# Layer 0's first modulation, norms and projections in a hand-written order with their loads, and the mLSTM gates issued behind the first queries

## The chip, the cores and the metric

The kernel runs on one core of one Trainium2 chip. The metric is the device time of one execution in microseconds (us), and of several executions the median is taken. Engines are named as the profile names them: PE multiplies matrices, DVE is the vector engine, ACT the scalar engine, POOL the GpSimd engine, SP issues the DMAs. PSUM is the accumulator memory of PE, in eight banks of 512 fp32 columns on 128 partitions.

## The reference, cut to what matters

Two layers of a transformer that is modulated by a conditioning vector work on 1024 latent tokens and 256 context tokens of width 1024. The change touches the beginning of layer 0 alone:

```python
mod_l = (jax.nn.silu(c) @ ada_w[layer] + ada_b[layer]).reshape(batch, 1, N_MOD, D_MODEL)
mod_c = (jax.nn.silu(c_ctx) @ ada_w[layer] + ada_b[layer]).reshape(1, 1, N_MOD, D_MODEL)
h_l = modulate(x, norm1_g[layer], mod_l, 0)      # rms_norm(x, g) * (1 + mod[1]) + mod[0]
h_c = modulate(ctx, norm1_g[layer], mod_c, 0)
y_c, y_l = ab_mixer(h_c, h_l, ab_w_in[j], ab_gate_b[j], mlstm_norm_g[j], swa_q_norm_g[j],
                    swa_k_norm_g[j], swa_sink[j], ab_w_out[j], not last)
```

`ab_mixer` projects the modulated tokens to mLSTM gates, mLSTM heads, and the queries, keys and values of a banded attention. An mLSTM gate is a running sum and a running maximum along the tokens.

## The kernel before, in words

**Layout and groups.** Activations lie with the channel on the partition: `x[j]`, j = 0 to 7, holds 128 channels of all 1280 tokens. Tokens go in three groups, 0 and 1 of 512 and 2 of 256. Every projection is done in about twice the precision of one pass: activation and weight are split in a high and a low part (`hhi`, `hlo`, and a weight's two halves), and three matmuls are added up per 128 channels (high by high, low by high, high by low). With three groups, eight chunks j and two weight units (G for the gates and KB for the keys) that is 96 matmuls of 512 columns and 48 of 256 in the first stage.

**The first stage**, `first` (L2246 to L2284), has four kinds of work.

- Modulation, `ada_quarter(q)` (L229): quarter q gives shift and scale of the chunks j = 2q and 2q+1. It loads four tiles of `ada_w` (two DMAs of 256 KB each, L241) into a ring of slots s0f to s5f called raw, multiplies them by the conditioning vector (L244), copies one half of the result out of PSUM on ACT (L249), adds the other on DVE (L251), turns the sums to the partition axis by 16 small matmuls (L255), and adds the bias and forms the scale `gs` on DVE (L262, L267). No chunk of a quarter can be modulated before its L267.
- Statistics, `norm_stats` (L306), per group: eight squares on ACT (L312), added up in a tree of five additions on DVE and two on POOL (L315), one matmul with ones (L300), then Ln and Exp on ACT (L302, L303), which give the reciprocal root `rs`.
- Modulated chunk, `norm_apply` (L356): DVE multiplies `x`, `gs` and `rs` (L364), ACT adds the shift and writes `hhi` (L369). For an even j DVE then writes `hlo` (L374); for an odd j ACT writes the full value (L371) and POOL subtracts (L372). The scratch of squares and chunks is one ring of five buffers.
- Projection (L2281): six matmuls per chunk.

The weight units come by L395 and are split by ACT (L378) and POOL (L379); a third unit, V, is split there too, into the tiles mrv and irv.

**What sets the order.** Both before and after, an engine executes its instructions in one fixed order and waits on semaphores. Before, the framework's scheduler chose that order for the whole kernel from the order in which the Python code issues the work. `first` issued four rounds q = 0 to 3: load and square group q, modulation quarter q, then all chunks that this quarter allows for the groups at hand.

**What comes next.** `mixer0` (L1218) goes on with the keys, the values, and then with the queries and the mLSTM heads, whose projections are L404 to L406, with evacuations at L449 (ACT), L450 (DVE) and L478 (DVE, after the squares' matmul L475). It issued `gates` (L1119) ahead of the first queries. `gates` computes its scans on DVE (L1156 to L1179), four exponentials per direction on ACT (L1197, L1199), and for each of the two directions 14 small matmuls into PSUM banks 3 and 5 (L1206 and L1211), each bank copied out by DVE (L1207, L1215) before it is filled again. L1382 is a score matmul of the attention.

Of the kernel before, what the change touches and what calls it, by code (L numbers as in the profile page):

```python
# [10 lines left out]
F32 = mybir.dt.float32  # L11
F32R = mybir.dt.float32r
# [7 lines left out]
P = 128  # L20
D = 1024
ND = D // P
CTX = 256
LAT = 1024
T = CTX + LAT
# [3 lines left out]
TGS = [(256, 512, 0), (768, 512, 0), (0, 256, 1)]  # L29
# [17 lines left out]
PG = 1024  # L47
# [49 lines left out]
class Kernel:  # L97
# [128 lines left out]
            )  # L226
        yield

    def ada_quarter(self, q, tp, psp):  # L229


        nc, a = self.nc, self.a
        acc = tp.tile([P, 512], F32, tag="adaacc")
        for kk in range(2):
            ps = psp.tile("D", "adaps")
            for e in range(2):
                w = tp.tile([P, 2, 2, 256], F32, tag="raw")
                k0 = 4 * kk + 2 * e
                src = a["ada_w"][0, k0 * P : (k0 + 2) * P, 0:2048].rearrange("(k p) (b n) -> p k b n", p=P, b=2)
                for b in range(2):  # L240
                    nc.sync.dma_start(w[:, :, b, :], src[:, :, b, q * 256 : q * 256 + 256])  # L241
                for i in range(2):
                    c = 2 * e + i
                    nc.tensor.matmul(  # L244
                        ps[32 * c : 32 * c + 32, :], self.cs[:, k0 + i, :], w[:, i, :, :].rearrange("p b n -> p (b n)"),
                        start=True, stop=True, tile_position=(0, 32 * c),
                    )
            if kk == 0:
                nc.scalar.activation(acc, ps, AF.Copy)  # L249
            else:  # L250
                nc.vector.tensor_tensor(acc, ps, acc, op=ALU.add)  # L251
        pt = psp.tile("D", "adapt")
        for i in range(4):
            for u in range(2):
                nc.tensor.matmul(  # L255
                    pt[:, 2 * i : 2 * i + 2], acc[:, i * P : (i + 1) * P], self.asel[:, 2 * u : 2 * u + 2],
                    start=u == 0, stop=u == 1,
                )
        j = slice(2 * q, 2 * q + 2)
        bc = lambda t: t.unsqueeze(2).to_broadcast([P, 2, 2])  # L260
        ab = self.v(V_AB, 16).rearrange("p (b i) -> p b i", b=2)[:, :, j]
        nc.vector.tensor_tensor(  # L262
            self.mod[0][:, :16, :].rearrange("p (b i) v -> p b i v", b=2)[:, :, j, :],
            pt[:, :8].rearrange("p (b i v) -> p b i v", b=2, v=2),
            ab.unsqueeze(3).to_broadcast([P, 2, 2, 2]), op=ALU.add,
        )
        nc.vector.scalar_tensor_tensor(  # L267
            self.gs[0, 1][:, j, :], self.mod[0][:, 8 + 2 * q : 10 + 2 * q, :], 1.0, bc(self.v(V_N1 + 2 * q, 2)),
            op0=ALU.add, op1=ALU.mult,
        )  # L270
# [947 lines left out]
    def mixer0(self, first):  # L1218
        nc, a = self.nc, self.a
        cp = self.cp  # L1220
        dr = self.pool(self.ctx, "dr0", space=DRAM)
        mixd = [dr.tile([P, T], F32, tag=f"m0_{k}", name=f"m0_{k}") for k in range(ND)]
        ud = [[dr.tile([P, T], F32, tag=f"u{h}{i}", name=f"u{h}{i}") for i in range(4)] for h in range(4)]
        tri = cp.tile([P, 2, P], BF16, tag="tri", name="tri")
        idb = cp.tile([P, P], BF16, tag="idb", name="idb")
        sel = cp.tile([P, 2, 8], F32R, tag="sel", name="sel")
        with ExitStack() as ctx:
            kp = self.pool(ctx, "kp", side="right")
            with ExitStack() as c2:
                sp = self.sp = self.pool(c2, "sp")  # L1230
                small = Area(sp.tile([P, 640], F32, tag="small", name="small"))
                wp = self.weights_ring((0, 1), (0, PG))
                gy, heads = first(wp, kp)
                psp = self.banks(A=(0, 1), B=(2, 3), Q=(4,), S=(5,))
                tp = self.area(6 * PG, 8 * PG)
                self.qt_bufs = 1
                tr = tp.tile([P, 512], F32, tag="qsw")[:, : 2 * P].rearrange("p (d q) -> p d q", d=2)
                nc.sync.dma_start(tr, a["tri"].rearrange("d p q -> p d q"))
                nc.vector.tensor_copy(tri, tr)
                nc.vector.tensor_copy(idb, self.ident)  # L1240
                selc = small.tile([P, 1], F32, tag="selc")
                for d in range(2):
                    for h in range(4):
                        k = d * 4 + h
                        r = 64 * d + h
                        nc.vector.tensor_tensor(
                            selc, self.ident[:, r : r + 1], self.ident[:, r + 32 : r + 33], op=ALU.add
                        )
                        for i in range(2):
                            nc.vector.tensor_scalar(sel[:, i, k : k + 1], selc, (-1.0, 1.0)[i], None, op0=ALU.mult)  # L1250
                tb = self.area(5 * PG, 6 * PG)
                psa = self.banks(A=(0, 1, 2), B=(7,), Q=(4,), G=(3, 5))
                st, qs = self.swa_setup(sp, tp, tb, psa, wp, heads, gy)
                mr, ir, cb, tq = self.gates(kp, small, psa, gy)
                for _ in st[-1](psa, 0, qs):
                    pass
                self.gps = self.banks(A=(6, 7))
                heads = [self.gather(wp, tb, ud, h) for h in range(4)]
                for _ in range(7):
                    next(heads[0])  # L1260
                self.gps = psp
                self.swa(sp, small, tb, psp, wp, mixd, heads, st, qs)
                keep = self.area(NF - 320)
                kept = []
                for t in (cb, tq):
                    k = keep.tile(list(t.shape), F32, tag=f"k{len(kept)}")
                    nc.vector.tensor_copy(k, t)
                    kept.append(k)
            self.stage_weights()
            self.mlstm(mr, ir, *kept, tri, idb, sel, mixd, ud)  # L1270
        hb = self.hb = self.pool(self.ctx, "hb", side="right").tile([P, 5 * H], F32R, tag="hb", name="hb")
        self.hid = Area()
        self.hid_places = cuts(self.hidA, H, 0, H, 2 * H) + cuts(hb, H, *(i * H for i in range(5)))
        self.hid.place("hid", self.hid_places)
        self.make_gs(0, 2)
        self.new_h()
        return self.out_proj0(mixd)
# [954 lines left out]
def body(ctx: ExitStack, tc: tile.TileContext, a, out):  # L2232
    nc = tc.nc
# [12 lines left out]
    def first(wp, kp):  # L2246
# [1 line left out]

        sl = [k.sp.tile([P, T], F32, tag=f"s{i}", name=f"s{i}f") for i in range(7)]
        tp = k.area(2 * PG)  # L2250
        tp.place("raw", [x[:, :PG] for x in sl[:6]])
        tp.place("adaacc", cuts(k.F, H, 6 * PG))
        ps = k.banks(N=(0, 1, 2), G=(0, 1, 2), K=(3, 5, 6), D=(4, 7))
        k.nrs_bufs, k.nt_bufs = 3, 5
        k.gs[0, 1] = k.cp.tile([P, ND, 2], F32, tag="gs01", name="gs01")
        rs, heads, w = {}, {}, []
        for q in range(4):
            if q < 3:
                k.load_x(a["x"], TGS[q : q + 1], 0)
                rs[q] = k.norm_stats(TGS[q], tp, ps, "N")  # L2260
            if q == 0:
                w = [k.unit(wp, a["win0"][u]) for u in (U_G, U_KB)]
                hl = [kp.tile([P, T], F32R, tag=x, name=x + "v")[:, :PG] for x in ("mr", "ir")]
                heads["v"] = k.unit(wp, a["win0"][U_VB], place=(k.F[:, 7 * PG : 8 * PG], *hl))
            k.ada_quarter(q, tp, ps)
            todo = [(i, 2 * q, 2 * q + 2) for i in range(min(q, 2))]
            if q < 3:
                todo.append((q, 0, 2 * q + 2))
            else:
                todo.append((2, 6, 8))  # L2270
            for i, j0, j1 in todo:
                k.norm_apply(TGS[i], rs[i], 0, 1, tp, range(j0, j1))
                t0, n, vv = TGS[i]
                if t0 not in heads:
                    heads[t0] = [ps.tile(x, "pj") for x in "GK"]
                for j in range(j0, j1):
                    c = slice(j * P, j * P + P)
                    hi, lo = (t[:, j, t0 : t0 + n] for t in (k.hhi, k.hlo))
                    for o, (wh, wl) in zip(heads[t0], w):
                        for m, (x, y) in enumerate(((wh, hi), (wh, lo), (wl, hi))):  # L2280
                            nc.tensor.matmul(  # L2281
                                o[:, :n], x[:, c], y, start=j == 0 and m == 0, stop=j == ND - 1 and m == 2
                            )
        return sl[6], heads  # L2284

    nt = k.area(5 * PG, NF)
# [41 lines left out]
```

## Time and profile before

| what | value |
|---|---|
| median of three runs | 2880.11 us (2876.76 to 2883.9) |
| the profiled execution | 2882.76 us, of which the span of the trace is 2881.0 us |
| granted TensorE clock, mean | 0.981 of full speed |
| instructions | 41902 |
| DMA traffic | 432.11 MB, mean 150 GB/s |

The page gives busy time per engine over the span; the timeline view gives start, duration, engine, line, operation and operands of single instructions, with the idle time ahead of them and what released them in brackets; the windows view gives busy time per stretch, in which PEclk is the granted clock. A few per cent of PE records can be missing.

### The profile page before, as it was taken

To read this page: it belongs to the slowest core of one execution; us is meant where nothing else is said; L and a number is where in the kernel's file an instruction comes from. 1 tells how busy PE (TensorE), PEld (TensorE's weight loads), DVE (VectorE), ACT (ScalarE), POOL (GpSimd) and SP (SyncE) were. 2 spreads that over 40 slices of the span, in tenths; PEclk is the share of its full clock that TensorE was granted. 3 is DMA by queue.
4 is the path that set the end of the run, shared out by engine and by line. 5 is a ranking of instruction groups with operands and counts; after the bars stand their busy time and mean duration, and the time that the engine had idled before them with its cause. 6 is when DMAs were issued, how large, how long until landed. Compare 5 with 4: busy or idle time off the path is not lost.

```text
span 2881.0 us, 41902 instructions
## 1 busy us (share of the span) xinstructions
PE 2745.3 (95%) x15174; PEld 2334.7 (81%) x15174; DVE 1992.4 (69%) x3285; ACT 1503.1 (52%) x2640; POOL 1160.9 (40%) x768
## 2 busy tenths in 40 slices
PE   6889999999898999989999998999989999999999
PEld 3678788878787888878878898999988888888877
DVE  5836555667869877746777836888885567766766
ACT  5555554445654334344346645888875555544332
POOL 3431220110326666550001654777775299840000
PEclk9889999999999999999999999999999999999999
DMA  6113223352324566669765831000026245577674
GB/s 231 61 50 103 79 97 136 112 194 80 119 92 136 179 210 212 201 211 332 244 208 161 264 124 32 27 19 27 20 77 218 88 150 199 189 254 270 213 226 154
DMA packets 200368, 432.11 MB, mean 150 GB/s; under 512 B 21216, under 2 KB 46944, under 8 KB 200160
## 3 DMA queue, kind: packets, MB, share of 16 engines
q1 hardware_dynamic: 200160, 429.43, 45.2%
q8 instruction: 119, 1.95, 0.3%
q14 instruction: 89, 0.73, 0.1%
HBM read 326.85 MB, written 102.50 MB: 149 GB/s over the span
## 4 chain that ended last, share of the span: by engine, by line
PE 55%; DVE 12%; DMA 8%; issue 7%; ACT 4%; POOL 4%; SPq 0%; DVEq 0%; POOLq 0%; ACTq 0%
PE psum L998 12%; PE psum L569 12%; DMA hhiraw<-in_w 4%; PE psum L406 4%; PE psum L404 4%; PE psum L405 4%; PE psum L1924 4%; PE psum L2112 3%; PE psum L1830 3%; DVE W L379 3%; POOL W L379 2%; DVE F L623 1%; DVE F L211 1%; PE psum L1091 1%; DVE x L1003 1%
## 5 line engine op out<-in xcount | busy, mean ns | idle before, releaser
L379 POOL TENSOR_TENSOR W<-F,W 128x512 fp32r<-128x512 f32 (+2 forms) x323 | 516.5, 1614 | 524.9 <-ACT W L378 398.3
L998 PE MATMUL psum<-W,W 128*128 128x512 f32 x2688 | 622.7, 393 | 14.5 <-DVE W L379 6.4
L998 PEld LDWEIGHTS psum<-W,W 128*128 128x128 f32 x2688 | 506.5, 189 | 130.4 <-DVE W L379 15.8
L569 PE MATMUL psum<-hhi,W 128*128 128x512 f32 (+1 forms) x1600 | 449.3, 361 | 16.3 <-DVE x L623 7.0
L378 ACT ACTIVATE W<-F 128x512 fp32r<-128x512 f32 (+2 forms) x380 | 273.7, 739 | 250.7 <-POOL F L542 98.4
L569 PEld LDWEIGHTS psum<-hhi,W 128*128 128x128 f32 x1600 | 289.5, 192 | 63.3 <-DVE x L623 8.8
L569 PE MATMUL psum<-hlo,W 128*128 128x512 f32 (+1 forms) x800 | 287.2, 359 | 0.0
L378 ACT ACTIVATE W<-hhiraw 128x1024 fp32r<-128x1024 f32 x98 | 103.9, 1061 | 326.3 <-PE psum L998 252.6
L404 PE MATMUL psum<-hhi,W 128*128 128x512 f32 (+1 forms) x624 | 233.0, 373 | 6.6 <-DVE F L478 6.6
L406 PE MATMUL psum<-hhi,W 128*128 128x512 f32 (+1 forms) x624 | 228.1, 366 | 1.3 <-POOL W L379 1.3
L405 PE MATMUL psum<-hlo,W 128*128 128x512 f32 (+1 forms) x624 | 227.8, 365 | 0.0
L924 DVE TENSOR_TENSOR hhiraw<-hhiraw 128x512 f32<-128x512 f32 x154 | 105.2, 689 | 127.0 <-DMA hhiraw<-in_w 120.2
L372 POOL TENSOR_TENSOR hlo<-F,hhi 128x512 fp32r<-128x512 f32 (+1 forms) x28 | 35.0, 1254 | 361.2 <-ACT F L371 357.4
L542 POOL TENSOR_TENSOR F<-F 128x512 f32<-128x512 f32 x112 | 170.2, 1520 | 17.4 <-DMA F<-in_w 10.3
L569 PEld LDWEIGHTS psum<-hlo,W 128*128 128x128 f32 x800 | 153.7, 192 | 21.5 <-issue 0.2
L379 DVE TENSOR_TENSOR W<-hhiraw,W 128x1024 fp32r<-128x1024 f32 x98 | 119.6, 1221 | 46.2 <-ACT W L378 46.1
L404 PEld LDWEIGHTS psum<-hhi,W 128*128 128x128 f32 x624 | 119.2, 191 | 27.4 <-DVE F L478 7.0
L406 PEld LDWEIGHTS psum<-hhi,W 128*128 128x128 f32 x624 | 118.9, 191 | 18.6 <-POOL W L379 1.7
L405 PEld LDWEIGHTS psum<-hlo,W 128*128 128x128 f32 x624 | 119.3, 191 | 16.9 <-issue 1.7
L569 PE MATMUL psum<-x,W 128*128 128x512 f32 x504 | 123.5, 390 | 0.0
L581 ACT ACTIVATE F<-F 128x512 f32<-128x512 f32 x82 | 51.3, 626 | 134.9 <-DVE F L623 134.9
L379 DVE TENSOR_TENSOR W<-hloraw,W 128x1024 fp32r<-128x1024 f32 x98 | 119.4, 1219 | 0.1
(432 smaller groups left out, 6533.3 us busy)
## 6 DMA issues: line engine op xcount, KB each, us to landing
F<-in_w SPq DMA_DIRECT2D x104, 512.0 KB, 4.4
hloraw<-hd SPq DMA_DIRECT2D x90, 512.0 KB, 4.8
hhiraw<-in_w SPq DMA_DIRECT2D x72, 512.0 KB, 4.1
hd<-F SPq DMA_DIRECT2D x142, 256.0 KB, 2.2
hhiraw<-in_w SPq DMA_DIRECT2D x116, 256.0 KB, 5.4
F<-in_ada_w SPq DMA_DIRECT2D x96, 256.0 KB, 3.3
hd<-x SPq DMA_DIRECT2D x90, 256.0 KB, 2.3
F<-in_win SPq DMA_DIRECT2D x33, 512.0 KB, 3.7
```

The source lines that it names most:

```text
L378: nc.scalar.activation(hi, src, AF.Copy)
L379: eng.tensor_tensor(lo, src, hi.bitcast(F32), op=ALU.subtract)
L404: nc.tensor.matmul(ps, sh, mh, start=i == 0, stop=False)
L405: nc.tensor.matmul(ps, sh, ml, start=False, stop=False)
L406: nc.tensor.matmul(ps, sl, mh, start=False, stop=i == n - 1)
L542: add = lambda o, p, q, how: nc.gpsimd.tensor_tensor(o, p, q, op=how)
L569: nc.tensor.matmul(ps, w[i][:, p], B[j][k], start=first and j == 0 and m == 0, stop=last and j == 3 and m == 2)
L924: tt = lambda o, p, q, how: eng.tensor_tensor(o, p, q, op=how)
L998: nc.tensor.matmul(bank(base + i), A[u][:, p], B[v], start=first and m == 0, stop=last and m == 2)
L1830: nc.tensor.matmul(ps, s[:, c], m[:, j, t0 : t0 + QT], start=j == 0 and i == 0, stop=j == ND - 1 and i == 2)
L1924: nc.tensor.matmul(u.o[:, :QT], v[x], p[y], start=c == 0 and m == 0, stop=c == 2 * NB - 1 and m == 2)
L2112: self.nc.tensor.matmul(ps, x[:, c], y, start=first and m == 0, stop=last and m == 2)
```

## The change

`ada_quarter` is split: `ada_load(i)` issues the two DMAs of tile i (i = 0 to 15), and `ada_quarter(q, ws)` does the rest with four tiles already issued. The raw ring has seven slots instead of six. The body of `first` stands under `manual_schedule` for all five engines, so that its instructions run in the order written. In `mixer0`, the call of `gates` moves from ahead of the first queries to behind them and behind seven steps of the first head's gathering. No computation is added or left out. The rest of the kernel is still ordered by the scheduler.

```diff
+        def load(n):
+            for _ in range(n):
+                tiles.append(k.ada_load(next(number), tp))
...
+        with k.tc.manual_schedule(engines={E.PE, E.DVE, E.Activation, E.Pool, E.SP}):
+            k.load_x(a["x"], TGS[:1], 0)
+            stats(0)
+            w = [k.unit(wp, a["win0"][u]) for u in (U_G, U_KB)]
+            load(7)
+            raw = k.F[:, 7 * PG : 8 * PG]
+            nc.sync.dma_start(raw, a["win0"][U_VB])
+            k.load_x(a["x"], TGS[1:2], 0)
+            ada(0)
+            load(4)
+            k.load_x(a["x"], TGS[2:], 0)
+            apply(0, 0, 2)
+            ada(1)
+            load(4)
+            project(0, 0, 2)
+            apply(0, 2, 4)
+            v = heads["v"] = [kp.tile([P, T], F32R, tag=x, name=x + "v")[:, :PG] for x in ("mr", "ir")]
+            k.split(*v, raw, nc.gpsimd)
+            project(0, 2, 4)
+            stats(1)
+            apply(1, 0, 4)
+            ada(2)
+            load(1)
+            project(1, 0, 4)
+            for i in range(2):
+                apply(i, 4, 6)
+                project(i, 4, 6)
+            stats(2)
+            apply(2, 0, 6)
+            ada(3)
+            project(2, 0, 6)
+            for i in range(3):
+                apply(i, 6, 8)
+                project(i, 6, 8)
...
                 st, qs = self.swa_setup(sp, tp, tb, psa, wp, heads, gy)
-                mr, ir, cb, tq = self.gates(kp, small, psa, gy)
                 for _ in st[-1](psa, 0, qs):
                     pass
                 self.gps = self.banks(A=(6, 7))
                 heads = [self.gather(wp, tb, ud, h) for h in range(4)]
                 for _ in range(7):
                     next(heads[0])
+                mr, ir, cb, tq = self.gates(kp, small, psa, gy)
```

Line numbers in the rows of after are five higher than before for the functions behind `ada_quarter` (L312 becomes L317, L1211 becomes L1216).

On ACT, in the first stage, the squares of group 1 (x_116 to x_123) stood before between the first chunks of group 0:

```order
L249 ACTIVATE F<-psum 128x512
L312 ACTIVATE F<-x_116 128x512
L312 ACTIVATE F<-x_117 128x512
L369 ACTIVATE hhi<-F,mod_80 128x512
L312 ACTIVATE F<-x_118 128x512
L369 ACTIVATE hhi<-F,mod_80 128x512
L312 ACTIVATE F<-x_119 128x512
L371 ACTIVATE F<-F,mod_80 128x512
```

They stand now behind the copy of the second quarter (the second L254), the chunks that need it, and the high part of V (mrv):

```order
L254 ACTIVATE F<-psum 128x512
L374 ACTIVATE hhi<-F,mod_80 128x512 x2
L376 ACTIVATE F<-F,mod_80 128x512
L383 ACTIVATE mrv<-F 128x1024
L317 ACTIVATE F<-x_116 128x512
L317 ACTIVATE F<-x_117 128x512
L317 ACTIVATE F<-x_118 128x512
```

So a square of group 1 runs only when quarter 1 is done and its two chunks of group 0 are written.

On PE, behind the last of the key projections, the small matmuls of the gates (L1206, L1211) stood before closely one after another, between query projections:

```order
L1206 MATMUL psum<-x_808,ident 128x10 x4
L1211 MATMUL psum<-ident,x_808 128x128 x8
L406 MATMUL psum<-hhi,W_104 128x512
L404 MATMUL psum<-hhi,W_104 128x512
L475 MATMUL psum<-F,blk 128x512
L405 MATMUL psum<-hlo,W_104 128x512
L406 MATMUL psum<-hhi,W_104 128x512
L1211 MATMUL psum<-ident,x_808 128x128 x2
L475 MATMUL psum<-F,blk 128x512
L1211 MATMUL psum<-ident,x_808 128x128 x2
L1206 MATMUL psum<-x_808,ident 128x10 x4
L1211 MATMUL psum<-ident,x_808 128x128 x8
```

They stand now some 120 matmuls later, and the query and head projections (L409 to L411) stand ahead of them; of their second direction this is the beginning:

```order
L1216 MATMUL psum<-ident,x_1120 128x128 x2
L1384 MATMUL psum<-KH_627,x_813 128x256
L1385 MATMUL psum<-KL_629,x_813 128x256
L1384 MATMUL psum<-KH_627,x_814 128x256
L1385 MATMUL psum<-KL_629,x_814 128x256
L409 MATMUL psum<-hhi,W_103 128x512
L1211 MATMUL psum<-x_1120,ident 128x10 x4
L1216 MATMUL psum<-ident,x_1120 128x128 x2
L410 MATMUL psum<-hlo,W_103 128x512
L411 MATMUL psum<-hhi,W_103 128x512
```

Between the first direction's transposes and these stand 24 projection matmuls. The number of instructions on each engine is the same in both programs, and the order of all engines is the same from PE's 684th matmul on (DVE's 209th instruction, ACT's 184th, POOL's 59th).

More of the change, by code (lines that the diff above doesn't have):

```diff
@@ L227, in ada_sums, with ada_load, ada_quarter @@
         yield
-    def ada_quarter(self, q, tp, psp):
-        nc, a = self.nc, self.a
+    def ada_load(self, i, tp):
+        q, k0 = i // 4, 2 * (i % 4)
+        w = tp.tile([P, 2, 2, 256], F32, tag="raw")
+        src = self.a["ada_w"][0, k0 * P : (k0 + 2) * P, 0:2048].rearrange("(k p) (b n) -> p k b n", p=P, b=2)
+        for b in range(2):
+            self.nc.sync.dma_start(w[:, :, b, :], src[:, :, b, q * 256 : q * 256 + 256])
+        return w
+    def ada_quarter(self, q, ws, tp, psp):
+        nc = self.nc
         acc = tp.tile([P, 512], F32, tag="adaacc")
@@ L236, in ada_quarter @@
             for e in range(2):
[L237 to L241, printed above, removed]
+                w, k0 = ws[2 * kk + e], 4 * kk + 2 * e
                 for i in range(2):
@@ L2250, in first @@
         tp = k.area(2 * PG)
-        tp.place("raw", [x[:, :PG] for x in sl[:6]])
+        tp.place("raw", [x[:, :PG] for x in sl])
         tp.place("adaacc", cuts(k.F, H, 6 * PG))
@@ L2255, in first @@
         k.gs[0, 1] = k.cp.tile([P, ND, 2], F32, tag="gs01", name="gs01")
[L2256 to L2283, printed above, removed]
@@ new lines, in first, with stats, ada, apply @@
+        rs, heads, tiles = {}, {}, deque()
+        number = iter(range(16))
+        def load(n):
+            for _ in range(n):
+                tiles.append(k.ada_load(next(number), tp))
+        def stats(i):
+            rs[i] = k.norm_stats(TGS[i], tp, ps, "N")
+        def ada(q):
+            k.ada_quarter(q, [tiles.popleft() for _ in range(4)], tp, ps)
+        def apply(i, j0, j1):
+            k.norm_apply(TGS[i], rs[i], 0, 1, tp, range(j0, j1))
+        def project(i, j0, j1):
+            t0, n, vv = TGS[i]
+            if t0 not in heads:
+                heads[t0] = [ps.tile(x, "pj") for x in "GK"]
+            for j in range(j0, j1):
+                c = slice(j * P, j * P + P)
+                hi, lo = (t[:, j, t0 : t0 + n] for t in (k.hhi, k.hlo))
+                for o, (wh, wl) in zip(heads[t0], w):
+                    for m, (x, y) in enumerate(((wh, hi), (wh, lo), (wl, hi))):
+                        nc.tensor.matmul(o[:, :n], x[:, c], y, start=j == 0 and m == 0, stop=j == ND - 1 and m == 2)
@@ new lines, in first @@
+        E = mybir.EngineType
+        with k.tc.manual_schedule(engines={E.PE, E.DVE, E.Activation, E.Pool, E.SP}):
[32 more added lines that the diff above has]
+                project(i, 6, 8)
```

## The prediction

> **What bounds the kernel now.** I read the page, then busy time by stretches of 20 us, then the single instructions of the first 216 us. That is all that the change reorders. The page:
>
> ```profile
> span 2881.0 us, 41902 instructions
> ...
> PE 2745.3 (95%) x15174; PEld 2334.7 (81%) x15174; DVE 1992.4 (69%) x3285; ACT 1503.1 (52%) x2640; POOL 1160.9 (40%) x768
> ```
>
> PE is the bound of the whole, and the profiled execution took 2882.76 us, 2.65 above the median of the runs shown (2880.11). I make the sum against the profiled execution, and take 2.65 off at the end. Stretches (start:end and length, then busy us of PE, PEld, DVE, ACT, POOL with instructions, granted clock, DMA share, GB/s):
>
> ```profile
> 20.00:40.00 20.00, 14.45 (x56) 6.47 (x50) 8.71 (x13) 9.22 (x16) 4.53 (x4) 0.83 1.05 346
> 80.00:100.00 20.00, 17.37 (x69) 13.26 (x70) 15.79 (x19) 16.93 (x24) 11.37 (x8) 0.83 0.35 111
> 120.00:140.00 20.00, 14.46 (x74) 11.81 (x72) 19.91 (x19) 10.06 (x14) 6.62 (x3) 0.97 0.03 13
> 180.00:200.00 20.00, 20.00 (x108) 16.89 (x107) 4.53 (x21) 7.20 (x18) 2.40 (x1) 1.00 0.26 90
> ```
>
> From 180 on PE has work all the time. So what the change does to the moment at which PE gets there goes to the end nearly whole. Before that, the first stage waits for loads (20 to 40: the DMA share is full), and after it for DVE (19.91 of 20 busy from 120 to 140).
>
> **First stage: a chain of four quarters.** The chunks of a quarter wait for its `gs` (L267). Its times before are these, with the last matmul tile and the last addition of quarter 0 ahead:
>
> ```profile
> 21.30 1.75 PE L244 MATMUL psum<-s3f,cs 128*32 128x512 f32 x4
> 23.15 0.69 DVE L251 TENSOR_TENSOR F<-psum,F 128x512 f32<-128x512 f32 x1 [9.53 <-ACT F L312]
> 26.09 0.16 DVE L267 SCALAR_TENSOR_TENSOR gs<-mod,vec 128x4 f32<-128x4 f32 x1
> 43.10 0.16 DVE L267 SCALAR_TENSOR_TENSOR gs<-mod,vec 128x4 f32<-128x4 f32 x1
> 59.50 0.16 DVE L267 SCALAR_TENSOR_TENSOR gs<-mod,vec 128x4 f32<-128x4 f32 x1
> 80.22 0.16 DVE L267 SCALAR_TENSOR_TENSOR gs<-mod,vec 128x4 f32<-128x4 f32 x1
> 89.43 2.39 ACT L449 ACTIVATE F<-psum 32x512 f32<-32x512 f32 x4
> ```
>
> So `gs` stood ready at 26.25, 43.26, 59.66 and 80.38, and ACT had evacuated the first finished projection (L449) at 91.82, 11.44 after the last `gs`. From a quarter's last tile on PE to its `gs` it is 26.25 - 21.30 = 4.95, and from the start of L251 it is 3.10. With the change, the four times come out as follows.
>
> *Quarter 0.* V's load is no longer ahead of the four tiles. It gains one or two us there, which nothing later uses: quarter 1 waits for its own load.
>
> *Quarter 1.* The last tile it needs (s0f's second use) is issued behind 8 loads of group 0, three weight units, seven tiles and 8 loads of group 1. Before, s1f had the same transfers ahead of it:
>
> ```profile
> 25.96 1.00 SPq L241 DMA_DIRECT2D s1f<-in_ada_w  x2
> s1f<-in_ada_w SPq DMA_DIRECT2D x4, 256.0 KB, 5.7
> ```
>
> Its second half is issued at 26.5 and lands 5.7 later, at 32.2 to 32.4. Add 4.95: `gs` 1 at 37.4, 5.9 earlier than before. This is the gain of the new order of loads.
>
> *Quarter 2.* It is behind the statistics of group 1 now. I take durations from the groups of lines (busy and mean ns of one in the first 95 us) and three single rows:
>
> ```profile
> L364 DVE SCALAR_TENSOR_TENSOR F<-x,gs,F 128x512 f32<-128x512 f32 x16 | 11.3, 748 | 3.6 <-ACT F L303 3.4
> L369 ACT ACTIVATE hhi<-F,mod 128x512 fp32r<-128x512 f32 x16 | 11.2, 720 | 16.0 <-DVE F L364 15.8
> L372 POOL TENSOR_TENSOR hlo<-F,hhi 128x512 fp32r<-128x512 f32 x8 | 11.3, 1414 | 39.7 <-ACT F L371 36.0 <-DVE F L364 3.7
> L312 ACT ACTIVATE F<-x 128x512 f32<-128x512 f32 x16 | 9.8, 626 | 5.9 <-DMA x<-in_x 4.7 <-POOL hlo L372 0.9
> L315 POOL TENSOR_TENSOR F<-F 128x512 f32<-128x512 f32 x4 | 5.1, 1266 | 11.2 <-ACT F L312 11.2
> L378 ACT ACTIVATE mrv<-F 128x1024 fp32r<-128x1024 f32 x1 | 1.0, 1047 | 0.0
> L379 POOL TENSOR_TENSOR irv<-F,mrv 128x1024 fp32r<-128x1024 f32 x1 | 2.4, 2363 | 0.0
> 13.67 2.08 PE L300 MATMUL psum<-F,ones 128*128 128x512 f32 x2 [13.67 <-DVE F L315]
> 31.45 1.70 ACT L312 ACTIVATE F<-x 128x512 f32<-128x512 f32 x3 [0.87 <-POOL hlo L372]
> 35.54 1.12 PE L300 MATMUL psum<-F,ones 128*128 128x512 f32 x2 [1.21 <-DVE F L315]
> 38.19 0.62 ACT L303 ACTIVATE F<-F 128x512 f32<-128x512 f32 x1
> ```
>
> Two chunks of group 0 follow `gs` 1: on DVE 0.75 (L364), 0.75 (L374, waiting for ACT's first 0.72) and 0.75 (L364), on ACT 0.72 and 0.71 (L371, as L369). ACT then does V's high part, 1.05: from 37.4 to 42.9. Only then come the squares of group 1, whose data landed more than ten us before. Eight take 5.0. POOL has V's low part (2.36) queued behind L372 and ahead of its two additions (1.27 each), and the ring of five buffers makes the later squares wait for these. So the tree ends near 51.2 rather than at 49.5. L300 finds PE idle, costs 2.08 as at 13.67 and not 1.12 as at 35.54, and Ln and Exp 1.3: `rs` of group 1 at 55.0, where before it was at 38.81. DVE then has six instructions of 0.75 and two of the rope tables (0.75 at least) for its four chunks. L374 waits for ACT once, and once for POOL (below). L251 starts near 62.3, and `gs` 2 comes at 65.4, 5.7 later than before.
>
> *Quarter 3.* It stands behind group 2's statistics and six of its chunks. Its data have long landed. DVE and POOL hold each other up where both read:
>
> ```profile
> 65.73 1.30 POOL L372 TENSOR_TENSOR hlo<-F,hhi 128x512 fp32r<-128x512 f32 x1 [13.15 <-ACT F L371]
> 65.74 4.70 DVE L364 SCALAR_TENSOR_TENSOR F<-x,gs,F 128x256 f32<-128x256 f32 x4
> 74.13 0.48 DVE L374 SCALAR_TENSOR_TENSOR hlo<-F,mod,hhi 128x256 fp32r<-128x256 f32 x1
> L312 ACT ACTIVATE F<-x 128x256 f32<-128x256 f32 x8 | 3.1, 412 | 3.1 <-POOL hlo L372 3.0
> ```
>
> Four 256-wide products beside POOL took 4.70 instead of 4 x 0.48 = 1.9. From `gs` 2, four chunks of 512 take six DVE steps of 0.75, ACT's first and last two (0.72 and 1.43), and about 2 of such waits: ACT ends at 74.0. Eight squares of 256 (3.3), the tree's end and L300 (about 2.3, as 2.4 before from the last square at 33.15 to 35.54 in group 1) and Ln and Exp at 0.9 give `rs` at 80.6. Six chunks need nine DVE steps of 0.48 (4.3), three waits for ACT and two for POOL (together about 4): L251 at 88.7, `gs` 3 at 91.8, 11.4 later than before.
>
> The tail is the same work in the same engine orders as before, 11.44; up to 14 with PE cold all along. I take 12.5: ACT ends at 104.3 instead of 91.82. **The first stage loses 12.5.**
>
> The rows that bear on "cold" are in the next part. The Trainium skill, "TensorE: Matmul & The Clock Gate", part 1 on the clock gate, says that an idle window of about 3.4 us halves the clock, and that 3.4 us of work win it back; by its figures, as an estimate, each of the four idle stretches of PE that the new order makes (ahead of quarters 1 to 3 and of L300) would cost 1.7, or 6.8 if all lay on the path, and the time would then be about 4 above my sum.
>
> **Second stage: the gates.** DVE's order from `gs` 3 to the first L478 is the same up to neighbours, and DVE is busy throughout, so its stall for PE stays and only shifts:
>
> ```profile
> 140.65 0.47 DVE L478 SCALAR_TENSOR_TENSOR F<-psum,vec,F 128x256 f32<-128x256 f32 x1
> 141.18 0.80 PE L404 MATMUL psum<-hhi,W 128*128 128x512 f32 x1 [6.62 <-DVE F L478]
> 145.61 0.41 PE L405 MATMUL psum<-hlo,W 128*128 128x512 f32 x1
> ```
>
> (Cold until 145.6, then 0.39 to 0.41 a matmul.) What changes is behind it, where PE now has query and head projections in place of the waits for the gates:
>
> ```profile
> 150.00:155.00 5.00, 3.62 (x15) 1.85 (x13) 3.07 (x11) 4.06 (x7) 2.32 (x2) 1.00 0.00 0
> 155.00:160.00 5.00, 1.31 (x5) 0.94 (x6) 1.39 (x2) 4.92 (x8) 0.11 (x1) 0.59 0.00 2
> 160.00:165.00 5.00, 3.37 (x15) 2.82 (x16) 2.93 (x11) 4.87 (x9) 3.55 (x2) 0.50 0.00 0
> 165.00:170.00 5.00, 5.00 (x22) 4.24 (x22) 2.08 (x3) 3.29 (x8) 2.60 (x3) 0.55 0.14 52
> 153.80 0.41 ACT L1197 ACTIVATE x<-x 4x256 f32<-4x256 f32 x1 [0.17 <-POOL x L1186]
> 158.46 0.66 PE L1211 MATMUL psum<-ident,x 128*128 128x128 f32 x2 [4.26 <-issue]
> ```
>
> PE is idle for 1.38 + 3.69 + 1.63 = 6.7 from 150 to 165. The 9.68 of work from 155 to 170 runs at a clock of 0.50 to 0.59, which costs about 4.3 more. That is 11.0. The transposes of the second direction wait for ACT's exponentials of it (from 153.80), which wait for the first direction's transposes. With 24 projection matmuls between the two directions (24 x 0.23 = 5.5) that chain is mostly covered. What stays in the new order: the attention's scores, now ahead, share bank 7 with the projections and wait for its evacuation (ACT and DVE, about 2.7), and two waits for the gates' own banks (about 1). **The second stage gains 11.0 - 3.7 = 7.3.** The bounds: 4 if the chain is covered only by half, 13.0 if nothing of it stays and the cold restart at 141.18 (4.4 at about half speed, 2.0 lost) goes too.
>
> **The sum.** 2882.76 + 12.5 - 7.3 = 2888.0 beside the profiled execution, 2885.3 beside the median: 5.2 slower, 0.2%. A difference under 0.3% (8.6 us) can't be told from none here.
>
> **Rivals.**
>
> *A. The order costs its full price (slower by far).* Every wait of DVE and POOL for each other falls badly and PE's tail is cold: the first stage ends at 110.5 instead of 91.82, a loss of 18.7, and the gates gain only 4, since ACT's exponentials are still awaited. That is +14.7: 2894.8. For it speaks the 4.70 for four products; against it that the 11.44 behind the last `gs`, with the same engines and such waits in it, is not far from what its DVE work takes alone: six steps of 0.75 and three of 0.48, 5.9, and then ACT's 2.4 and PE's last chunks. It decides when `gs` 3 is later than about 95. Chance 0.23.
>
> *B. The chain runs without these waits (faster).* If POOL's V part, two waits at 512 and two at 256 for POOL, and the cold L300 cost nothing (3.6 + 2.6 + 2.0 + 1.0 = 9.2), the first stage loses 3.3; with the gates' full 13.0 that is -9.7: 2870.4. For it: the loads really are 5.9 earlier. Against: POOL's queue is in the order written, so V's part must run ahead of the additions. It decides when `gs` 3 comes before 84. Chance 0.12.
>
> *C. The beginning doesn't reach the end.* If a later wait on loads absorbs the shift, the time is 2880.1. Against it stand 20.00 of 20 busy from 180 on. Chance 0.05.
>
> *D. Both parts gain or lose less than I think, and cancel:* first stage +7, gates -7: 2880. Chance 0.06. That the change doesn't do what it says is excluded by the instruction orders.
>
> **How the numbers follow.** The forecast has 0.54, between 2881 and 2891; by the last of that, beyond 2888.7, 0.11 is slower by over 0.3%. With A, slower has 0.34. Faster has B's 0.12. The rest, 0.54, is within 0.3%. The range reaches from near B's price, 2871, to somewhat beyond A's, 2897.
>
> **What would show it.** In the profile of the changed kernel: `gs` (L272) near 24.8, 37.4, 65.4 and 91.8; the first square of group 1 near 42.9, not by 26; ACT's L454 done near 104; idle PE ahead of `gs` 2 and `gs` 3; the stall ahead of L478 shifted by some 12; and the rows of the gates without idle PE of more than 3 us at a time. I would be wrong if `gs` 2 comes before 60 (then the squares of group 1 didn't wait), or if PE idles behind the gates as long as before.

## The result and the profile after

The changed kernel takes 2896.18 us in the median of six runs (2890.33 to 2899.87), the kernel before 2880.38 (six runs, 2876.65 to 2883.9). The ratio is 1.0056, with a 95% interval of 1.0044 to 1.0068: about 16 us slower. A second measurement on another occasion gave 1.0053 (1.0038 to 1.0067). The profiled execution took 2899.05 us. Its page has the same work:

```profile
span 2897.2 us, 41899 instructions
...
PE 2746.4 (95%) x15174; PEld 2338.9 (81%) x15174; DVE 1984.9 (69%) x3285; ACT 1502.5 (52%) x2640; POOL 1157.2 (40%) x768
```

PE's busy time is 1.1 us longer and the span 16.2, so the loss is idle PE. The same stretches of 20 us as before:

```profile
20.00:40.00 20.00, 12.01 (x55) 6.53 (x54) 4.03 (x8) 2.90 (x5) 4.82 (x3) 0.63 1.05 353
80.00:100.00 20.00, 10.74 (x56) 7.78 (x54) 7.42 (x15) 8.59 (x21) 7.37 (x8) 0.75 0.03 8
140.00:160.00 20.00, 15.85 (x80) 12.93 (x78) 19.91 (x22) 8.61 (x14) 5.05 (x3) 1.00 0.13 50
180.00:200.00 20.00, 19.57 (x99) 16.70 (x99) 3.56 (x3) 8.89 (x12) 6.50 (x5) 1.00 0.28 88
```

From 80 to 100, where before ACT was busy for 16.93 and DVE for 15.79, no engine is busy for more than 11 us. Every engine waits for another there. The stretch in which DVE is full (19.91) has moved from 120 to 140 to a later place, 140 to 160. The timeline of the changed kernel has the stations of the chain:

```profile
24.86 0.16 DVE L272 SCALAR_TENSOR_TENSOR gs<-mod,vec 128x4 f32<-128x4 f32 x1
27.13 1.00 SPq L235 DMA_DIRECT2D s0f<-in_ada_w  x2
36.23 3.58 PE L260 MATMUL psum<-asel,F 128*128 128x2 f32 x16 [0.85 <-DVE F L256]
40.05 0.16 DVE L272 SCALAR_TENSOR_TENSOR gs<-mod,vec 128x4 f32<-128x4 f32 x1
45.56 2.70 ACT L317 ACTIVATE F<-x 128x512 f32<-128x512 f32 x5
54.22 2.08 PE L305 MATMUL psum<-F,ones 128*128 128x512 f32 x2 [6.06 <-DVE F L320]
57.72 0.75 DVE L369 SCALAR_TENSOR_TENSOR F<-x,gs,F 128x512 f32<-128x512 f32 x1 [3.55 <-ACT F L308]
66.77 0.69 DVE L256 TENSOR_TENSOR F<-psum,F 128x512 f32<-128x512 f32 x1 [2.02 <-ACT F L254]
67.51 3.57 PE L260 MATMUL psum<-asel,F 128*128 128x2 f32 x16 [7.86 <-DVE F L256]
71.32 0.16 DVE L272 SCALAR_TENSOR_TENSOR gs<-mod,vec 128x4 f32<-128x4 f32 x1
96.47 3.57 PE L260 MATMUL psum<-asel,F 128*128 128x2 f32 x16 [8.99 <-DVE F L256]
100.28 0.16 DVE L272 SCALAR_TENSOR_TENSOR gs<-mod,vec 128x4 f32<-128x4 f32 x1
112.75 1.79 ACT L454 ACTIVATE F<-psum 32x512 f32<-32x512 f32 x3
161.31 1.73 PE L480 MATMUL psum<-F,blk 128*128 128x512 f32 x2 [4.72 <-ACT F L451]
163.48 0.79 PE L409 MATMUL psum<-hhi,W 128*128 128x512 f32 x1 [0.44 <-DVE F L483]
233.23 1.07 PE L174 MATMUL psum<-F,cs 128*32 128x512 f32 x8
```

The four `gs` are ready at 25.02, 40.21, 71.48 and 100.44 (before 26.25, 43.26, 59.66, 80.38), and ACT ends its first evacuation at 114.54 (before 91.82). That is 22.7 later. PE's first matmul behind L478 (L483 now) starts at 163.48 instead of 141.18, 22.3 later. The stall ahead of it is as long as before: from the end of the projection ahead of it PE runs no other for 6.88 us, before for 6.62 (the squares' matmuls L480, for which DVE waits, fall in between). L174, the first matmul of the modulation that comes next, stands in the same place of both orders: 233 instructions of DVE, 212 of ACT and 60 of POOL run ahead of it in either. Before, it stands at

```profile
218.97 1.06 PE L174 MATMUL psum<-F,cs 128*32 128x512 f32 x8
```

so the second stage has given 22.3 - 14.3 = 8.0 back. The remaining 14.3 go to the end, where 16.2 are found; the two in between are within what executions differ by (last section). Of DVE's waits in the first 115 us, these three come to the most in the changed kernel, and the kernel before has the third of them but once:

```profile
DVE F L256 <- PE psum L249: 15.0, 2, 7.6
DVE mod L267 <- PE psum L260: 13.0, 4, 3.7
DVE hlo L379 <- ACT hhi L374: 11.2, 11, 1.6
```

Before:

```profile
DVE hlo L374 <- ACT hhi L369: 2.0, 1, 2.0
```

The columns are us in all, times, and the longest. Eleven times DVE stands still between a chunk's product and its subtraction, until ACT has written `hhi`, for 9.2 us more than before.

### The profile page after: what moved, and what is told of

It is laid out like the page before. It is cut to its first block, busy times and chain, and to the rows that moved or that the text cites. A ratio compares the mean times of both kernels' runs of the same rounds, so it can differ in the third digit from the quotient of the medians.

```text
span 2897.2 us, 41899 instructions
## 1 busy us (share of the span) xinstructions
PE 2746.4 (95%) x15174; PEld 2338.9 (81%) x15174; DVE 1984.9 (69%) x3285; ACT 1502.5 (52%) x2640; POOL 1157.2 (40%) x768
## 3 DMA queue, kind: packets, MB, share of 16 engines
q8 instruction: 119, 1.95, 0.3%
## 4 chain that ended last, share of the span: by engine, by line
PE 58%; DVE 12%; DMA 6%; issue 6%; ACT 3%; POOL 3%; SPq 0%; DVEq 0%; POOLq 0%; ACTq 0%
PE psum L1003 13%; PE psum L574 13%; PE psum L1929 4%; PE psum L409 4%; PE psum L411 4%; PE psum L410 4%; DMA hhiraw<-in_w 3%; PE psum L2117 3%; PE psum L1835 3%; DVE W L384 2%; POOL W L384 2%; PE psum L1096 2%; DVE F L628 1%; DVE F L211 1%; DVE x L1008 1%
## 5 line engine op out<-in xcount | busy, mean ns | idle before, releaser
L409 PE MATMUL psum<-hhi,W 128*128 128x512 f32 (+1 forms) x624 | 232.1, 372 | 2.0 <-ACT F L1359 1.6
L411 PE MATMUL psum<-hhi,W 128*128 128x512 f32 (+1 forms) x624 | 227.3, 365 | 1.3 <-POOL W L384 1.3
L409 PEld LDWEIGHTS psum<-hhi,W 128*128 128x128 f32 x624 | 118.9, 190 | 23.6 <-ACT x L383 2.5
L411 PEld LDWEIGHTS psum<-hhi,W 128*128 128x128 f32 x624 | 118.6, 190 | 18.6 <-POOL W L384 1.7
```

Of the source, the lines that this page charges most:

```text
L409: nc.tensor.matmul(ps, sh, mh, start=i == 0, stop=False)
L411: nc.tensor.matmul(ps, sl, mh, start=False, stop=i == n - 1)
```

## The experiments

My theory after the result: two parts that add up, a first stage that costs 22 us and gates that give back 8. Of the first stage I held three causes for possible: the statistics' place, a cold PE, and DVE's waits for ACT. The rivals stand with each run. Each ratio is to runs of the kernel before on the same occasion.

**The gates alone.** The kernel before, with the call moved:

```diff
-                mr, ir, cb, tq = self.gates(kp, small, psa, gy)
                 for _ in st[-1](psa, 0, qs):
                     pass
...
                     next(heads[0])
+                mr, ir, cb, tq = self.gates(kp, small, psa, gy)
```

> The first stage is that of before, only the gates are issued behind the first queries. My theory (the two parts add up; the first stage costs about 22 us and the gates give back about 8, read off the two traces at PE's L404 behind L478, 141.18 against 163.48, and at its first L174, 218.97 against 233.23): about 8 us faster than before, 2872. Rival (the 8 us were given back only because PE had come late to that place, so that the gates' scans had time to finish): no more than 3 us faster, 2877 or above.

Measured: 2873.64 us, ratio 0.998 (0.997 to 0.999), 3 to 9 us faster. The rival's 3 us is at the edge of the interval. In the trace L174 stands at 213.95, 5.0 earlier than before. PE's waits from 135 to 214 in this kernel:

```profile
PE psum L475 <- ACT F L446: 5.0, 1, 5.0
PE psum L404 <- ACT F L1354: 3.1, 2, 2.7
...
PE psum L1211 <- issue: 0.2, 1, 0.2
```

The stall of the key projection stays (now put down to ACT's copy ahead of it), and the 4.3 that PE waited for the gates have become 0.2. A new wait of 3.1 for an evacuation (L1354) takes part of it.

**The first stage alone.** The changed kernel with that call put back (the diff above, reversed).

> The first stage is the hand-written one, the gates are issued ahead of the first queries as before. My theory: about 22 us slower than before, 2902, and ACT's first L454 done near 114.5 as in the changed kernel. Rival (the scheduler would have hidden a part of the later start behind the gates anyway): 14 to 17 us slower, as the changed kernel.

Measured: 2905.32 us, ratio 1.0084 (1.007 to 1.0098), 20 to 28 slower. The rival is out, and L174 stands at 241.52, 22.6 later than before. The gates' wait is back in PE's waits from 160 to 232:

```profile
PE psum L1216 <- ACT x L1202: 5.4, 1, 5.4
PE psum L409 <- DVE F L483: 5.4, 1, 5.4
```

The two parts add up: 0.9980 + 1.0084 - 1 = 1.0064, beside 1.0056. At L174 it is 22.6 - 5.0 = 17.6, beside 14.3; single marks scatter by about 2 (last section).

**A PE kept busy.** The changed kernel with spare matmuls on PE where it waits in quarters 1 to 3 and for the sums of group 1's squares. Their result lands in a bank that the first projection of group 2 overwrites:

```diff
+        def spin(n):
+            for _ in range(n):
+                nc.tensor.matmul(idle, w[0][0][:, :P], k.hhi[:, 0, TGS[0][0] : TGS[0][0] + 512], start=True, stop=True)
...
+                if kk and e and pre:
+                    spin(pre)
...
+        if post:
+            spin(post)
         pt = psp.tile("D", "adapt")
```

> The changed kernel with spare matmuls on PE while it waits in the first stage (17 in quarter 1, 18 ahead of the ones matmul of group 1, 24 and 30 in quarters 2 and 3; their result is overwritten). Theory that the cold clock is a part of the cost: the matmuls L260 take 1.95 instead of 3.58 three times, L305 of group 1 takes 1.12 instead of 2.08, L249 1.05 instead of 1.92, in all 6 to 9 us faster than the changed kernel, 2887 to 2890. Rival (the order alone costs it, a cold PE is hidden behind DVE and ACT): within 2 us of the changed kernel.

Measured: 2896.7 us, ratio 1.0056 (1.0043 to 1.0068), by the time no gain. In the trace the last `gs` came at 95.54, 4.9 earlier, though the transposes (L260) of quarter 1 still took 3.41. So I ran it again beside the changed kernel itself:

> The changed kernel itself, beside the others of this group on one chip: 2896 within 3 us, about 16 slower than before.

> The same kernel as e3_warm, with the changed kernel beside it. In the trace of e3_warm the last gs came at 95.54 instead of 100.44 and PE's first L174 at 227.7 instead of 233.2, and yet the median was that of the changed kernel. If the 5 us of the trace are real and the equal medians were scatter, it is 3 to 6 us faster than the changed kernel here; if something behind the first stage takes them back, it is again within 2 us of it.

Measured: 2895.41 us, 1.0053 (1.0038 to 1.0067), for the changed kernel, and 2891.29 us, 1.0041 (1.0027 to 1.0056), with the spare matmuls. In this second trace all transposes are short (L264 is L260 there), and L174 comes 7.6 earlier than at 233.23:

```profile
34.84 1.95 PE L264 MATMUL psum<-asel,F 128*128 128x2 f32 x16
63.61 1.95 PE L264 MATMUL psum<-asel,F 128*128 128x2 f32 x16 [2.02 <-DVE F L258]
91.00 1.95 PE L264 MATMUL psum<-asel,F 128*128 128x2 f32 x16 [1.99 <-DVE F L258]
93.19 0.16 DVE L276 SCALAR_TENSOR_TENSOR gs<-mod,vec 128x4 f32<-128x4 f32 x1
225.65 1.06 PE L174 MATMUL psum<-F,cs 128*32 128x512 f32 x8
```

So a cold PE is a cost on the path of the first stage: the transposes alone are 3.58 against 1.95, three times (4.9), and the last `gs` comes 7.1 earlier than in the first trace of the changed kernel (6.7 than in the second). In the time a gain is not shown: by the ratios it is nothing in the first pair and 3 to 4 us in the second, and both pairs of intervals overlap.

**Statistics of group 1 earlier.**

```diff
             apply(0, 0, 2)
+            stats(1)
             ada(1)
...
             project(0, 2, 4)
-            stats(1)
             apply(1, 0, 4)
```

> The changed kernel with one line moved: the statistics of group 1 ahead of quarter 1. Theory that quarter 2 is late because the squares of group 1 wait behind quarter 1, its chunks and V's high part: rs of group 1 is ready near 40 instead of 57.7, quarter 1 comes some 4 us later (44) since its addition is queued behind the statistics' additions, and the four chunks of group 1 start near 48.5 instead of 57.7, so about 9 us faster than the changed kernel, 2887. Rival (POOL's queue and the ring of five buffers are what hold up the statistics wherever they stand): no more than 3 us.

Measured: 2888.53 us, ratio 1.0029 (1.0018 to 1.0041). The later quarters:

```profile
45.39 0.16 DVE L272 SCALAR_TENSOR_TENSOR gs<-mod,vec 128x4 f32<-128x4 f32 x1
65.62 0.16 DVE L272 SCALAR_TENSOR_TENSOR gs<-mod,vec 128x4 f32<-128x4 f32 x1
94.66 0.16 DVE L272 SCALAR_TENSOR_TENSOR gs<-mod,vec 128x4 f32<-128x4 f32 x1
107.11 1.79 ACT L454 ACTIVATE F<-psum 32x512 f32<-32x512 f32 x3
```

Quarter 1 is 5.3 later, somewhat more than expected, and quarters 2 and 3 and the end of the stage are 5.6 to 5.7 earlier. So the statistics' place cost about 6 of the 22.7 in the trace. In the time it is about 8 (1.0029 against 1.0056), nearer to the 9 expected than to the rival's 3; beside the second measurement of the changed kernel (1.0053, from 1.0038 on) the intervals overlap by a little.

**Quarter 3 earlier as well.**

```diff
+            ada(3)
             stats(2)
             apply(2, 0, 6)
-            ada(3)
             project(2, 0, 6)
```

> e4_stats1_early with quarter 3 ahead of the statistics and chunks of group 2. Theory that quarter 3 was late only for its place behind them: its gs comes near 78 to 80 instead of 94.8, but the statistics and six chunks of group 2 then stand behind it, and the first stage ends 3 to 6 us earlier than in e4_stats1_early: 2883 to 2886. Rival (the sum of DVE's and ACT's work between quarter 2 and the end sets the end, whatever the place of quarter 3): within 2 us of e4_stats1_early, 2888.

Measured: 2889.73 us, ratio 1.0034 (1.0023 to 1.0046): the rival. The last `gs` comes 11.4 earlier, and the stage ends 0.9 earlier:

```profile
83.25 0.16 DVE L272 SCALAR_TENSOR_TENSOR gs<-mod,vec 128x4 f32<-128x4 f32 x1
106.17 1.79 ACT L454 ACTIVATE F<-psum 32x512 f32<-32x512 f32 x3
```

So what sets the end there isn't when quarter 3 is ready. That it is the chunks is my reading of it, and not DVE's and ACT's work in them alone: from 83 to 107 each of the two is busy for 13 us of 24, and much of the rest is waiting.

**A whole new order by hand.** Matmuls of each quarter first, its addition later, statistics early, V late. In it, `begin(q)` issues a quarter's matmuls and the first copy, and `next(s)` the addition, the transposes and `gs`. The beginning of its core:

```diff
+            apply(0, 0, 2)
+            project(0, 0, 2)
+            s = begin(1)
+            load(4)
+            stats(1)
+            next(s)
+            apply(0, 2, 4)
+            project(0, 2, 4)
+            s = begin(2)
+            load(1)
+            apply(1, 0, 2)
+            next(s)
```

> The hand-written stage in another order (each quarter's matmuls issued first and its addition later, squares of groups 1 and 2 ahead of the chunks that can't start yet, V's split late, first chunks projected ahead of quarter 1), the gates moved as in the changed kernel. Theory that the order of squares and quarters is what costs the first stage: gs near 24.8, 41, 50 and 57, ACT's first L454-like evacuation done at 78 to 82 instead of 91.8 before and 114.5 in the changed kernel, and the time 2858 to 2868. Rival (DVE and POOL holding each other up, and a cold PE, are what costs it, in any fixed order): first stage no shorter than before, 2873 or above.

Measured: 2893.11 us, ratio 1.0048 (1.0035 to 1.0061). My theory failed here, and clearly. The rows:

```profile
35.28 0.60 ACT L254 ACTIVATE F<-psum 128x512 f32<-128x512 f32 x1 [5.86 <-PE psum L249]
48.34 0.16 DVE L272 SCALAR_TENSOR_TENSOR gs<-mod,vec 128x4 f32<-128x4 f32 x1
82.91 0.16 DVE L272 SCALAR_TENSOR_TENSOR gs<-mod,vec 128x4 f32<-128x4 f32 x1
109.32 1.79 ACT L455 ACTIVATE F<-psum 32x512 f32<-32x512 f32 x3
40.00:60.00 20.00, 14.58 (x46) 8.36 (x46) 5.74 (x10) 5.39 (x9) 1.99 (x2) 0.50 0.32 102
```

ACT's copy of quarter 1 waits for matmuls that stand behind projections on PE, and the squares stand behind that copy. From 40 to 60 PE runs at half its clock, and DVE and ACT are busy for little over a quarter of the time. The time and the end of the stage (111.11) are as the rival had them. How much of that is DVE and POOL holding each other up, how much the low clock and how much the waits at such hand-overs was not told apart.

**The waits of DVE for ACT.** The changed kernel, in which DVE forms the product of the next chunk ahead of the subtraction for the one before:

```diff
             nc.scalar.activation(h, t[:, :n], AF.Identity, bias=sh)
+            while late:
+                late.popleft()()
             if j % 2:
...
             else:
-                nc.vector.scalar_tensor_tensor(lo, t[:, :n], sh, h.bitcast(F32), op0=ALU.add, op1=ALU.subtract)
+                late.append(lambda lo=lo, t=t, sh=sh, h=h: nc.vector.scalar_tensor_tensor(
+                    lo, t[:, :n], sh, h.bitcast(F32), op0=ALU.add, op1=ALU.subtract
+                ))
```

> The changed kernel with one difference: in each group of chunks DVE forms the product of the next chunk (L369) before it subtracts for the one before (L379), so that it need not wait for ACT's hhi in between. In the changed kernel these waits are 11 and 11.2 us in all up to 115, in before none. Theory that they are a large term of what I sized too small (I had counted one per group of chunks): 5 to 9 us faster than the changed kernel, 2887 to 2890, and the wait of L379 for hhi gone from DVE's waits. Rival (DVE would wait for something else instead, the next statistics or POOL): within 2 us of the changed kernel, 2895.

Measured: 2887.8 us, ratio 1.0042 (1.0028 to 1.0055). Of the 11.2 us of these waits 0.5 are left, in three. (Before, there had been one of 2.0, and not none.) ACT ends its first evacuation at 105.38, 9.2 earlier:

```profile
67.98 0.16 DVE L272 SCALAR_TENSOR_TENSOR gs<-mod,vec 128x4 f32<-128x4 f32 x1
92.90 0.16 DVE L272 SCALAR_TENSOR_TENSOR gs<-mod,vec 128x4 f32<-128x4 f32 x1
102.99 2.39 ACT L461 ACTIVATE F<-psum 32x512 f32<-32x512 f32 x4
```

At the end of the stage this is the largest single cause in the traces; at the last `gs` (7.4) it is level with the spare matmuls. In the time it is 3 to 4 us by the ratios, with overlapping intervals, so there a gain is not shown.

**The order left to the scheduler.** The changed kernel's code, same order of issue, seven slots and loads ahead, without the fixed order:

```diff
-        with k.tc.manual_schedule(engines={E.PE, E.DVE, E.Activation, E.Pool, E.SP}):
+        if True:
```

> The changed kernel's code in its order of issue, with seven slots and loads ahead, but without the fixed order: the scheduler orders the engines. Theory that fixing the order in units of whole groups of chunks costs the time, not the order of loads: the first evacuation by ACT ends by 92 to 96 as before instead of 114.5, and with the gates moved the time is 2870 to 2876. Rival (the order of issue itself, statistics late, decides whoever orders): 2885 or above.

Measured: 2873.61 us, ratio 0.9985 (0.9975 to 0.9994). Against 1.0056 with the fixed order that is 20 us. The first stage:

```profile
37.78 0.16 DVE L272 SCALAR_TENSOR_TENSOR gs<-mod,vec 128x4 f32<-128x4 f32 x1
79.72 0.16 DVE L272 SCALAR_TENSOR_TENSOR gs<-mod,vec 128x4 f32<-128x4 f32 x1
88.94 2.39 ACT L454 ACTIVATE F<-psum 32x512 f32<-32x512 f32 x4
```

Quarter 1 is ready 5.3 earlier than in the kernel before, thanks to the loads, and yet the stage ends at 91.33, where it ended at 91.82. So the earlier loads bring nothing that reaches the end of the stage. The time isn't told apart from that of the gates alone (0.998). Two costs of the fixed order are gone in this trace: DVE waits for `hhi` twice, 2.2 us in all, and the four groups of transposes take 1.84 to 2.05 each. The run frees all five engines at once; which engine's fixed order costs the time isn't shown.

**The repairs together**, in a fixed order: statistics of group 1 ahead of quarter 1, quarter 3 ahead of group 2, V's split behind group 2's first chunks, and the skew (the three diffs above, and the two lines of V moved).

> The fixed order with three repairs: statistics of group 1 ahead of quarter 1, quarter 3 ahead of group 2's statistics, V's split late, and the skewed order of e7_skew in every group of chunks. If the repairs add up (e6_ada3_early 6 and V about 3 and skew 5 to 9 below the changed kernel): 2876 to 2882, about the time of before. Rival (PE's clock stays low in any such order, since PE idles at each group): 2885 or above, with a granted clock of 0.5 to 0.75 from 40 to 100.

Measured: 2880.79 us, ratio 1.001 (1.0001 to 1.0018), with the end of the first stage at 99.22. The four repairs take about 13 us off the changed kernel's time, with intervals well apart. At the end of the stage it is 15.3, near the sum of the single steps (5.6, 0.9 and 9.2).

```profile
75.24 0.16 DVE L272 SCALAR_TENSOR_TENSOR gs<-mod,vec 128x4 f32<-128x4 f32 x1
96.83 2.39 ACT L461 ACTIVATE F<-psum 32x512 f32<-32x512 f32 x4
```

**The same code, left to the scheduler** (the one-line diff of the unpinned run on top).

> The order of issue of e9_combined, left to the scheduler as in e8_unpinned. If the order of issue still counts under the scheduler, as it did under the fixed order (e9_combined some 14 below the changed kernel): a few us faster than e8_unpinned, 2866 to 2871. Rival (the scheduler arrives at nearly the same from either): within 2 us of e8_unpinned, 2872 to 2876.

Measured: 2872.05 us, ratio 0.9975 (0.9966 to 0.9984): faster than both kernels, and not told apart from the gates alone (0.998) or from the unpinned order (0.9985). The rival holds: the scheduler comes to nearly the same from either order of issue.

## Why the prediction came out as it did

The time lies inside the range of 2871 to 2897, near its upper end. The forecast was 5.2 slower, within 0.3%, and about 16 slower came. The case that came, slower by over 0.3%, had 0.34. The signs of both terms were right, and one size was off. That the time lies inside the range is owed to rival A, whose price drew its upper end; the sum itself was 11 too low.

**The gates: gain 7.3 forecast, 8.0 in the traces.** Alone they bring 3 to 9 us, and under the hand-written first stage about 8 (1.0084 against 1.0056). The forecast of which wait would go and that DVE's stall ahead of L478 would only shift (by some 12; it shifted by 22.3) was right. So were the sizes behind it: from the end of that stall to L174 PE is idle for 4.7 us instead of 7.7, where I had 6.7 - 3.7 = 3.0 less, and busy for 65.1 instead of 70.1, at a granted clock of 0.96 instead of 0.88, where I had 4.3.

**The first stage: loss 12.5 forecast, 22.7 measured.** This term failed. By its own steps:

- *Quarter 1 at 37.4; it came at 40.21.* I had taken the issue of its last tile at 25.96, and it was 27.13 (1.2). I had taken 4.95 from the last tile to `gs` from quarter 0, and in it 1.95 for the transposes; PE had idled for the load, and they took 3.58 (1.6).
- *Quarter 2 at 65.4; it came at 71.48.* Inherited 2.8, cold transposes once more 1.6, and the rest behind `rs` of group 1: from 57.72 to L256 it took 9.05, where I had 7.3. The chunks themselves took 7.0 with their waits, so "L374 waits for ACT once, and once for POOL" was enough. What I had left out is that ACT's copy (L254), which L256 adds to, stands behind ACT's work for these chunks: DVE waits 2.02 for it.
- *Quarter 3 at 91.8; it came at 100.44.* 6.1 inherited, 1.6 cold transposes, 0.9 for the same copy (a wait of 1.60, with chunks that were a little quicker than I had). Up to `rs` of group 2 the step was right: 15.1 from `gs` 2, where I had 15.2.
- *The tail of 12.5; it took 14.1,* my upper bound.

So of the 10.2 that were missing, the cold transposes are 4.9, the waits for ACT's copy about 2.6, the tail 1.6, the load 1.2. The waits for `hhi`, the largest cost of the fixed order, are not among them: the sum had them (about 1.3, 2 and 4 us, with those for POOL), and what I expected of the skewed run, that I had counted one per group, misread it. Of a cold PE the sum held L300 and a share of the tail; further restarts it named only as an estimate (6.8 for four, of which about 2 were in the sum) beside it, and it gave no reason to leave the others out. L260 lies on the path itself: DVE waits for PE at each L267 (13.0 in all). The Trainium skill's rule of the clock gate ("TensorE: Matmul & The Clock Gate", part 1) fits what came: transposes behind idle stretches of 7.86 and 8.99 took 3.57, and 1.95 where spare matmuls filled most of these. It was the right rule, and it belonged in the sum.

**The rivals.** A (slower, 2894.8) had the time almost right and the threshold, `gs` 3 later than 95, too, but not all of the mechanism: it had the first stage lose 18.7 and the gates gain 4, and both are larger. B is out, as the quarters' times show, and C too: L174 is 14.3 later and the end 16.2. D is out as well: the first stage lost 22.7, not 7.

What the forecast called the order's price was, as the runs show, the price of fixing it: the same order of issue costs nothing when the scheduler interleaves (0.9985). That its units, whole groups of chunks, were too large is not shown; the order with smaller ones cost nearly as much (1.0048). Of the causes inside, the waits of DVE for ACT (9.2 at the end of the stage), the place of the statistics (5.6) and the cold PE (7.1 at the last `gs`) were each shown by a run, in its trace. In the time the four repairs together are clear, the statistics' place nearly so, the other two not. The four repairs end the stage 15.3 earlier, still 7.4 behind the order of before, though the last `gs` is 5.0 ahead of it (75.40 against 80.38). What these 7.4 consist of was not tested. The cold PE is a candidate, since that run has no spare matmuls: by stretches of 20 us the granted clock from 20 to 100 is 0.66 to 0.84 in it, and 0.83 to 0.91 before.

## What to carry to other kernels

In a hand-written order, a producer and a consumer on two engines must not stand back to back: put the next unit's first step between an instruction and the one that waits for another engine's answer to it, or every unit pays the round trip (9.2 us in this trace). Work whose data are there early (squares, sums) belongs ahead of work that waits for a load, and an idle matrix engine costs its clock as well, also where its few small matmuls lie on the other engines' path. Before fixing an order by hand, run the same order of issue under the scheduler: that one run would have separated the good half of this change from the bad one.

## What the runs showed that I had not expected

- Sixteen matmuls of two columns (L260) take 1.95 us behind a busy PE and 3.57 to 3.58 behind idle stretches of PE. I had expected so small an operation to be set by latency and not by the clock.
- Executions of one kernel scatter by more than some of these effects: the changed kernel's two profiled executions had L174 at 233.2 and 232.8, and spans of 2897.2 and 2885.5. So 11.3 of the 11.7 us of difference arise behind the part that the change touches, and an effect of 3 to 5 us is easier to see at a mark in the trace than in a median of six runs.
- Marks scatter as well. L174 of the two runs with spare matmuls is 2.1 apart (227.72 and 225.65), and with the gates alone the first stage, in the order of before, ended at 93.96 instead of 91.82. In both pairs the later one had cold transposes in quarter 1 (3.41 against 1.95 and 1.88), so a difference of 2 us at a mark says nothing yet.
- Bringing a load forward by several us (quarter 1 at 37.94 instead of 43.26) left no trace at the end of the same stage (91.33 against 91.82).
